# First adaLN sets loaded by feature blocks, and the first four column tiles accumulated as the blocks arrive

## The chip, the cores and the metric

One core of a Trainium2 chip runs the whole program. The metric is the device time of one execution in microseconds, the median of several runs. Two kernels compute the same outputs from the same inputs, and the second differs from the first by one change.

## The reference, cut to what matters

Two layers (`DEPTH = 2`) of a hybrid block with 1024 features run over 256 context tokens and 256 latent tokens. The host passes weights in float32.

```python
for l in range(DEPTH):
    mod = jax.nn.silu(c) @ ada_w[l] + ada_b[l]
    mod_c = jax.nn.silu(c_ctx) @ ada_w[l] + ada_b[l]
    sh1, sc1, g1, sh2, sc2, g2 = jnp.split(mod[:, None, :], 6, axis=-1)
    ...
    h = rms_norm(x, norm_gains[l, 0]) * (1.0 + sc1) + sh1
    hc = rms_norm(xc, norm_gains[l, 0]) * (1.0 + sc1c) + sh1c
    y, y_c = token_mixer(h, hc, ...)
```

`token_mixer` multiplies `h` by `w_in` (1024 x 6576). Columns of the product feed four mixers: a neighbourhood attention (NA), a latent attention (MLA), a gated DeltaNet (GDN) and an S5 state space; the remaining 4096 columns are gates. Each mixer's output is projected, multiplied by its sigmoid gate and summed (`merge_branches`), and a dense MLP follows. Nothing of `h` exists before the first two adaLN sets of the layer, shift `sh1` and scale `sc1`, are known. Each is a product of a conditioning vector with a 1024 x 1024 piece of `ada_w[0]`, for the context and for the latents.

## The kernel before, in words

Context and latents lie side by side as 512 columns (2 x 256), with features on 128 partitions in 8 feature tiles. A **column tile** is 128 columns of `w_in`; its product takes 24 matmuls of 512 columns: 8 feature tiles, and for each three products of split float32 (`mm3`: `whi*hhi`, `whi*hlo`, `wlo*hhi`), accumulated in one PSUM bank. Weights come by DMA as 512 KB `wstage` (3 buffers), ScalarE casts `whi`, VectorE subtracts `wlo` (4 buffers of each). `MIX_ORDER` fixes the order of column tiles in layer 0: u0, u1 (S5's input), nq0, nq1, nk0, nk1, nva, nvb, misc, then eight GDN tiles zipped with gate tiles, the rest of the gates, and MLA's. They are numbered from 0 below, so nk0 is tile 4.

All DMAs named here are issued by SyncE's queue (SP), in program order, and an SP entry that waits holds those behind it. Each other engine runs its own list in order too. Generators (S5's tables, S5, attention, GDN) are advanced by `tick` between column tiles; a scheduler then fixes each engine's list from priorities (`tc.high_priority()` raises one). So the lists below are fixed before the program runs.

**Front.** `first_dma` loads the first two adaLN sets as 16 pieces `ada1` (512 KB, rows of 128 input features each), between them `x` and the constants. `run_ada` accumulates the 8 pieces of a set into one bank (`ada_mm`), and `ada_end` transposes the sum into `mod` and `fac`. So scale, the second set, is there only after the 16th piece. `s5_tables` runs beside it on VectorE (512-column products `raw`, `t`, `sto`), GpSimd (a chain of powers `ph`) and SP. Then `make_h` makes h for the 256 context tokens over all 8 feature tiles, and after that for the 256 latents: VectorE `hb`, ScalarE `hhi`, VectorE `hlo` for each piece of 256 columns.

**Tiles 0 to 3.** `dense_group` takes u0 and u1 in two halves of 256 columns, following the halves of h; the PSUM pool `psd` has two buffers, emptied by ScalarE (`us`, L1425). nq0 and nq1 follow at 512 columns.

**S5.** `ct,bb` matmuls (L717, eight groups) finish the tables in steps; `U,sti` matmuls feed S5's input to its state; VectorE scans it (`tn`, `X`, L998); SP then loads `s5s` (S5's output maps, written to DRAM before by the table code as `s_dr`); `U,s5s` and `Q,s5s` matmuls give its output. Without waits at the list they stand between column tiles on TensorE.

**End of GDN.** The merges of `MERGE = [3, 0, 1, 2]` run over branches S5 (3), NA (0), MLA (1), GDN (2), 8 tiles a branch. GDN's steps (`cv`, `sR,N`, `svn,QK` matmuls with VectorE between) are spread over the gate tiles and merges. Before branch 2 come a sum `oo`, its norm on ScalarE (Square, a table load, Ln, Exp), transposes (L1344) and `yh`. Gates return by DMA into `gin` (3 buffers), ScalarE takes their tanh, VectorE multiplies by the projection, GpSimd adds to `macc`. `NA_AT = [6, 12]` is the number of gate tiles after which a layer's attentions begin to be emitted.

## Time and profile before

| | |
|---|---|
| times of three runs | 1705.52, 1707.88, 1708.6 us, median 1707.88 |
| profiled execution | 1704.83 us, of which the span is 1703.0 |
| mean granted TensorE clock | 0.962 of full speed |
| busy, share of the span | TensorE 93%, VectorE 63%, ScalarE 47%, GpSimd 13% |
| chain that ended last | TensorE 76%, VectorE 10%, DMA 7%, ScalarE 3% |

TensorE's weight loads overlap its matmuls and are listed as PEld. In the page's slices of the span TensorE shows 6 tenths in the first slice, 9 in most, and 7 in the slice that holds the end of layer 0's GDN. A timeline row has start, duration, engine, line, operation and, in brackets, the idle time before it with what ended it.

### The profile page before, as it was taken

The page shows a single profiled execution, that of the slowest core. Times are in us where ns is not written, and L with a number is a line of the kernel's source. Part 1 is how long each engine was busy: PE and PEld are TensorE (multiplying, and loading weights), DVE is VectorE, ACT ScalarE, POOL GpSimd, SP SyncE. Part 2 cuts the span into 40 slices and gives each one's busy share as a digit, 9 for nine tenths or more (in the row PEclk, how much of TensorE's full clock was granted, in tenths as well). Part 3 has the DMA queues.
Part 4 walks back from the last instruction along what each step waited for, and adds up shares of the span by engine and source line. Part 5 has one row for each costly group of instructions (what it writes and reads, how often), then busy time and mean ns, then how long its engine had stood idle before and what let it go on. Part 6 is the DMA issues. An engine that isn't in the chain of part 4 may idle for free.

```text
span 1703.0 us, 25390 instructions
## 1 busy us (share of the span) xinstructions
PE 1591.6 (93%) x9616; PEld 1321.3 (78%) x9616; DVE 1075.1 (63%) x1942; ACT 802.2 (47%) x1491; POOL 221.2 (13%) x316
## 2 busy tenths in 40 slices
PE   6699999999999888999999999789999998889996
PEld 2588777766778778878777878589998877779996
DVE  8766544574456767746757676756677557665554
ACT  5444456533334344534334453556545434556553
POOL 6830000000001454000010050100000002000000
PEclk9799999999999889999999999899999999889998
DMA  8456533445346523346545765334677316736652
GB/s 328 144 140 203 170 124 96 127 155 164 96 136 214 187 98 127 102 137 195 179 136 180 223 188 153 117 105 123 207 241 199 97 38 192 234 114 184 187 186 81
DMA packets 135915, 268.42 MB, mean 158 GB/s; under 512 B 38129, under 2 KB 76017, under 8 KB 135665
## 3 DMA queue, kind: packets, MB, share of 16 engines
q1 hardware_dynamic: 135792, 266.80, 50.1%
q8 instruction: 75, 1.23, 0.3%
q14 instruction: 48, 0.39, 0.1%
HBM read 234.02 MB, written 32.74 MB: 157 GB/s over the span
## 4 chain that ended last, share of the span: by engine, by line
PE 76%; DVE 10%; DMA 7%; ACT 3%; issue 2%; POOL 1%; SPq 0%; POOLq 0%; ACTq 0%; DVEq 0%
PE pd L215 40%; PE pm L215 24%; PE pg L215 9%; DVE wlo L204 2%; DMA gin<-g_dr 2%; DMA wstage<-in_ada 2%; PE pm L833 1%; DMA wstage<-in_win 1%; ACT whi L222 1%; DVE hlo L207 1%; POOL macc L204 1%; PE pd L378 1%; DVE aacc L207 1%; DMA s5s<-s_dr 1%; DMA ys<-yb_dr 1%
## 5 line engine op out<-in xcount | busy, mean ns | idle before, releaser
L204 DVE TENSOR_TENSOR wlo<-wstage,whi 128x1024 fp32r<-128x1024 f32 x264 | 327.4, 1241 | 244.0 <-ACT whi L222 236.0
L222 ACT CAST whi<-wstage 128x1024 fp32r<-128x1024 f32 x264 | 276.3, 1048 | 414.1 <-PE pd L215 163.1
L215 PE MATMUL pd<-hhi,whi 128*128 128x256 f32 (+1 forms) x1184 | 411.1, 348 | 22.7 <-ACT us L1425 10.0
L215 PE MATMUL pd<-hlo,whi 128*128 128x256 f32 (+1 forms) x1184 | 406.0, 343 | 2.8 <-DVE hlo L207 2.8
L215 PE MATMUL pd<-hhi,wlo 128*128 128x256 f32 (+1 forms) x1184 | 406.4, 344 | 0.0
L215 PEld LDWEIGHTS pd<-hhi,whi 128*128 128x128 f32 x1184 | 228.2, 193 | 61.2 <-ACT us L1425 10.2
L215 PEld LDWEIGHTS pd<-hlo,whi 128*128 128x128 f32 x1184 | 228.0, 193 | 33.5 <-issue 6.3
L215 PEld LDWEIGHTS pd<-hhi,wlo 128*128 128x128 f32 x1184 | 227.8, 192 | 31.5 <-issue 8.2
L215 PE MATMUL pm<-hhi,whi 128*128 128x256 f32 (+1 forms) x352 | 115.4, 328 | 5.6 <-ACT hhi L201 5.6
L215 PE MATMUL pm<-hlo,whi 128*128 128x256 f32 (+1 forms) x352 | 115.9, 329 | 2.6 <-DVE hlo L207 2.5
L215 PE MATMUL pm<-hhi,wlo 128*128 128x256 f32 (+1 forms) x352 | 114.7, 326 | 0.0
L207 DVE SCALAR_TENSOR_TENSOR aacc<-wstage,csl,aacc 128x1024 f32<-128x1024 f32 x63 | 81.9, 1320 | 19.8 <-DMA wstage<-in_ada 19.7
L215 PE MATMUL pd<-fhi,whi 128*128 128x256 f32 (+1 forms) x272 | 90.5, 333 | 2.4 <-DVE y L204 2.4
L215 PE MATMUL pd<-fhi,wlo 128*128 128x256 f32 (+1 forms) x272 | 90.4, 332 | 1.2 <-DVE wlo L204 1.2
L215 PE MATMUL pm<-fhi,whi 128*128 128x256 f32 (+1 forms) x272 | 90.1, 331 | 0.0
L215 PE MATMUL pd<-flo,whi 128*128 128x256 f32 (+1 forms) x272 | 90.0, 331 | 0.0
L215 PE MATMUL pm<-flo,whi 128*128 128x256 f32 (+1 forms) x272 | 89.4, 329 | 0.2 <-DVE flo L204 0.2
L215 PE MATMUL pm<-fhi,wlo 128*128 128x256 f32 (+1 forms) x272 | 89.3, 328 | 0.0
L215 PEld LDWEIGHTS pm<-hhi,whi 128*128 128x128 f32 x352 | 68.6, 195 | 13.6 <-ACT hhi L201 6.8
L215 PEld LDWEIGHTS pm<-hlo,whi 128*128 128x128 f32 x352 | 68.1, 194 | 9.6 <-DVE hlo L207 3.7
L215 PEld LDWEIGHTS pm<-hhi,wlo 128*128 128x128 f32 x352 | 68.1, 193 | 5.0
L215 PEld LDWEIGHTS pd<-fhi,whi 128*128 128x128 f32 x272 | 51.9, 191 | 7.7 <-issue 2.8
(588 smaller groups left out, 2881.9 us busy)
## 6 DMA issues: line engine op xcount, KB each, us to landing
wstage<-in_w SPq DMA_DIRECT2D x128, 512.0 KB, 4.2
wstage<-in_win SPq DMA_DIRECT2D x104, 512.0 KB, 4.1
wstage<-in_ada SPq DMA_DIRECT2D x80, 512.0 KB, 3.6
ada<-in_ada SPq DMA_DIRECT2D x16, 512.0 KB, 10.6
g_dr<-gt SPq DMA_DIRECT2D x32, 256.0 KB, 4.2
gin<-g_dr SPq DMA_DIRECT2D x16, 512.0 KB, 4.4
wstage<-in_wb SPq DMA_DIRECT2D x16, 512.0 KB, 4.1
wstage<-in_wout SPq DMA_DIRECT2D x16, 512.0 KB, 3.8
```

Source lines behind the costliest of these rows:

```text
L204: return (eng or V).tensor_tensor(o, a, b, op=op)
L207: return (eng or V).scalar_tensor_tensor(o, a, s, b, op0=op0, op1=op1)
L215: return PE.matmul(o, l, r, start=st, stop=sp)
L222: S.copy(hi, src)
L378: PE.matmul(ps[32 * q:32 * q + 32, 0:256], lhs, w[:, 256 * q:256 * q + 256], start=st, stop=sp)
L833: PE.transpose(ps[:, 128 * b:128 * b + 128], P[qt][:, 128 * b:128 * b + 128], ident)
```

## The change

The host passes a second copy of the two sets, `ada0`: 8 blocks of 1 MB. Block t holds shift and scale of feature tile t, for all 1024 input features. `cond_block(t)` multiplies a block by the conditioning vectors (8 matmuls into four partition quarters, 256 columns), copies the result on ScalarE (`ade`), adds the quarters and turns them by two matmuls with `sel2`, and two small VectorE instructions write `mod` and `fac` of tile t alone. So h can be made feature tile by feature tile, both halves at once, and `make_h` is called so. Tiles 0 to 3 (`NPRE`) get their PSUM banks early and take their three matmuls of a feature tile once it is there, with a lag (`LAG`) of 0, 0, 1 and 2 feature tiles. `x` is now loaded first; the S5 constants `bct` behind the first block and two `wstage`; five buffers hold blocks. The constants `cst` come in two loads. `NA_AT` goes from 6 to 10 in layer 0. After the layer's merges the order of TensorE's list is nearly the same in both.

```diff
+    a0 = g["ada_w"][0, :, 0:2048].reshape(8, 128, 2, 8, 128)
+    o["ada0"] = a0.transpose(3, 1, 0, 2, 4).reshape(8, 128, 2048)
...
-NA_AT = [6, 12]
+NA_AT = [10, 12]
...
-        jobs = [("ada", 0, 8 * s + k) for s in (0, 1) for k in range(8)]
+        jobs = []
...
-            if j < 16:
-
-                if k == 0:
-                    acc_a[0] = ada_ps()
-                ada_mm(acc_a[0], cs[:, k, :], w, k == 0, k == 7)
-                if k == 7:
-                    ada_end(l, s, acc_a[0])
-            elif (l, s) in ((0, 2), (0, 3), (0, 4), (1, 5)):
+            w = stage.pop(j)
...
-            for t in range(8):
+            for t in tiles:
...
-        first = {}
-        def first_dma(n):
-            while n and len(first) < 16:
-                j = len(first)
-                first[j] = px.tile([128, 1024], F32, name="ada1", tag="ada1", bufs=13)
-                SP.dma_start(first[j], I["ada"][0, jobs[j][2]])
-                n -= 1
+        SP.dma_start(smp, I["smp"].rearrange("l p n -> p l n"))
         xt = px.tile([128, 8, 512], F32, name="xt")
-        first_dma(1)
-        SP.dma_start(smp, I["smp"].rearrange("l p n -> p l n"))
+        for c0 in (0, 256):
+            SP.dma_start(xt[:, :, c0:c0 + 256], I["x"][:, :, c0:c0 + 256])
+        SP.dma_start(cst[:, 0:C_BONE], I["cst"][:, 0:C_BONE])
+        blocks = []
+        def block_dma():
+            t = px.tile([128, 8, 256], F32, name="adab", tag="adab", bufs=5)
+            SP.dma_start(t.rearrange("p k f -> p (k f)"), I["ada0"][len(blocks)])
+            blocks.append(t)
+        def cond_block(t):
+            w = blocks[t]
+            ps = ada_ps()
+            for k in range(8):
+                q = k % 4
+                PE.matmul(ps[32 * q:32 * q + 32, 0:256], cs[:, k, :], w[:, k], start=k < 4, stop=k >= 4)
+            e = px.tile([128, 256], F32, name="ade", tag="ade", bufs=2)
+            S.copy(e, ps[:, 0:256])
+            ps = ada_ps()
+            for s in range(2):
+                PE.matmul(ps[:, 2 * s:2 * s + 2], e[:, 128 * s:128 * s + 128], sel2, start=True, stop=True)
+            b = smp[:, 0, P_AB + t:P_AB + t + 16:8]
+            tt(mod[0][:, 0:2, t], ps[:, 0:4].rearrange("p (s c) -> p s c", s=2), b[:, :, None].to_broadcast([128, 2, 2]), ADD)
+            stt(fac[0][:, 0, t], mod[0][:, 1, t], 1.0, smp[:, 0, P_G + t:P_G + t + 1].to_broadcast([128, 2]), ADD, MUL)
...
+        block_dma()
+        issue_dma()
+        issue_dma()
         next(tables)
-        first_dma(1)
-        SP.dma_start(cst, I["cst"][:, 0:C_RO])
-        first_dma(2)
-        SP.dma_start(xt[:, :, 0:256], I["x"][:, :, 0:256])
-        first_dma(2)
-        SP.dma_start(xt[:, :, 256:512], I["x"][:, :, 256:512])
-        first_dma(7)
+        block_dma()
+        issue_dma()
+        block_dma()
...
+        tab = ln_table()
+        rs = []
+        with tc.high_priority():
+            for c0, n, sel in halves(0):
+                rs.append(x_rstd(xt, c0, n, px, tab))
+            sel2 = small.tile([128, 2], F32, name="sel2", tag="sel2", bufs=1)
+            V.tensor_reduce(sel2, ident.rearrange("p (q c) -> p c q", q=4)[:, 0:2, :], axis=AX, op=ADD)
         next(tables)
-        rs = []
-        tab = ln_table()
-        for j in range(16):
-            run_ada(j, first[j])
-            first_dma(1)
-            if j in (5, 9):
-                c0, n, sel = halves(0)[len(rs)]
+        NPRE, LAG = 4, (0, 0, 1, 2)
+        pre = {}
+        for t in range(8 + 1 + max(LAG)):
+            if t < 8:
                 with tc.high_priority():
-                    rs.append(x_rstd(xt, c0, n, px, tab))
-            if j > 5:
-                next(tables)
-        pos[0] = nstage[0] = nsplit[0] = 16
-        for _ in range(3):
-            issue_dma()
-        for c0, n, sel in halves(0):
-            with tc.high_priority():
-                make_h(0, xt, rs[sel], 0, c0, n, sel, px)
+                    cond_block(t)
+                    for c0, n, sel in halves(0):
+                        make_h(0, xt, rs[sel], 0, c0, n, sel, px, (t,))
+            for i in range(NPRE):
+                k = t - 1 - LAG[i]
+                if k == 0:
+                    prep_to(i)
+                    pool_, nm_ = (psd, "pd") if i < 2 else (psm, "pm")
+                    pre[i] = pool_.tile([128, 512], F32, name=nm_, tag=nm_)
+                if 0 <= k < 8:
+                    whi, wlo = parts[i]
+                    mm3(pre[i], whi[:, 128 * k:128 * k + 128], wlo[:, 128 * k:128 * k + 128],
+                        hhi[:, k], hlo[:, k], k == 0, k == 7)
+            while len(blocks) < min(8, t + 4):
+                block_dma()
+            if t == 6:
+                SP.dma_start(cst[:, C_BONE:], I["cst"][:, C_BONE:C_RO])
+            next(tables)
+        for i in range(NPRE):
+            parts.pop(i)
+        pos[0] = NPRE
...
+                ps = pre.pop(order.index(j)) if l == 0 and order.index(j) in pre else dense(key, hhi, hlo, n)
...
+                elif nm == "u0" and l == 0:
+                    for i in range(2):
+                        ps = pre.pop(i)
+                        for sel in range(2):
+                            store_u(i, sel, ps[:, 256 * sel:256 * sel + 256])
```

**TensorE while h is being made.** Before, 256-column matmuls of one tile after the other (`pd`), with S5's `ct,bb` among them:

```order
L215 MATMUL pd<-hhi,wlo 128x256
L717 MATMUL pm<-ct,bb 32x240 x4
L215 MATMUL pd<-hhi,whi 128x256
L215 MATMUL pd<-hlo,whi 128x256
L215 MATMUL pd<-hhi,wlo 128x256
L215 MATMUL pd<-hhi,whi 128x256
L215 MATMUL pd<-hlo,whi 128x256
L215 MATMUL pd<-hhi,wlo 128x256
```

Now, for one feature tile, tiles 0 and 1 (`pd`) and 2 and 3 (`pm`) in turn at 512 columns; `raw` belongs to S5's tables, `sel_313,ade` to a block:

```order
L1370 MATMUL pg<-sel_313,ade 128x2 x2
L671 MATMUL pm<-cst,raw 128x128 x4
L218 MATMUL pd<-hhi,whi 128x512 x2
L218 MATMUL pm<-hhi,whi 128x512 x2
L218 MATMUL pd<-hlo,whi 128x512
L218 MATMUL pd<-hhi,wlo 128x512
L218 MATMUL pd<-hlo,whi 128x512
L218 MATMUL pd<-hhi,wlo 128x512
L218 MATMUL pm<-hlo,whi 128x512
L218 MATMUL pm<-hhi,wlo 128x512
L218 MATMUL pm<-hlo,whi 128x512
L218 MATMUL pm<-hhi,wlo 128x512
```

The four tiles now advance together, and behind VectorE's last `hlo` stand eight matmuls of 512 columns until tile 4; before, 24 matmuls of 256 columns for each of u0 and u1, and then the whole of tiles 2 and 3, stood behind the last pieces of h. The first group of `ct,bb` moved from the start of tile 0 to a place just ahead of the eighth feature tile.

**TensorE at S5's input.** Before, the first of two groups of `U,sti` stands in tile 7:

```order
L215 MATMUL pd<-whi,hhi 128x256
L717 MATMUL pm<-ct,bb 32x240
L215 MATMUL pm<-U,sti 128x64 x16
L717 MATMUL pm<-ct,bb 32x240 x3
L215 MATMUL pd<-wlo,hhi 128x256
```

Now both groups stand at the end of tile 10:

```order
L218 MATMUL pd<-hhi,whi 128x512
L709 MATMUL pm<-ct,bb 32x240
L218 MATMUL pm<-U,sti 128x64 x16
L709 MATMUL pm<-ct,bb 32x240 x3
L218 MATMUL pd<-hlo,whi 128x512
L218 MATMUL pd<-hhi,wlo 128x512
L218 MATMUL pd<-hhi,whi 128x512
L218 MATMUL pd<-hlo,whi 128x512
L218 MATMUL pd<-hhi,wlo 128x512
L218 MATMUL pm<-U,sti 128x64 x16
L709 MATMUL pm<-ct,bb 32x240 x4
```

Counted in column tiles of 24 matmuls, the first group moved from 7.40 to 10.79 and the second from 7.96 to 11.0. The first group of `Q,s5s` moved from 12.67 to 13.0. SP's first `s5s` load waits in both lists for the last `X` of VectorE's scan. Ahead of tile 4 of the new list stands one of the eight `ct,bb` groups, and five more stand between there and the first `U,sti`.

**ScalarE at the end of layer 0's GDN.** Before, the norm follows the last gate's tanh with one table load:

```order
L201 ACTIVATE gin<-gin 128x1024 x2
L201 ACTIVATE oo_3394<-oo_3393 128x1024
L247 ACT_TABLE_LOAD
L201 ACTIVATE orr<-orr,kc 128x16
L201 ACTIVATE orr<-orr 128x16
L222 CAST yh<-ring 128x512 x2
L222 CAST whi<-wstage 128x1024
```

Now a gate's tanh (`gin`) stands between the Square of `oo` and the norm:

```order
L204 ACTIVATE gin<-gin 128x1024
L204 ACTIVATE oo_3375<-oo_3374 128x1024
L250 ACT_TABLE_LOAD
L204 ACT_TABLE_LOAD
L204 ACTIVATE gin<-gin 128x1024
L204 ACT_TABLE_LOAD
L204 ACTIVATE orr<-orr,kc 128x16
L204 ACT_TABLE_LOAD
L204 ACTIVATE orr<-orr 128x16
L225 CAST yh<-ring 128x512 x2
L225 CAST whi<-wstage 128x1024
```

There are four table loads where one was, and three of them stand behind the DMA that loads that gate. Of GDN's matmuls behind the merges of branches 3, 0 and 1, 8 `cv`, 8 `sR,N` and 8 more (4 and 4) `svn,QK` moved ahead of the last of those merges; 4 `svn,QK` are left behind it. In the front, ScalarE has seven table loads where it had three.

## Rows read from the trace of the kernel before

**Rows 1.** Engine line of the page, then ten-microsecond windows: engines' busy time (instructions), clock, DMA
```profile
PE 1591.6 (93%) x9616; PEld 1321.3 (78%) x9616; DVE 1075.1 (63%) x1942; ACT 802.2 (47%) x1491; POOL 221.2 (13%) x316
...
50.00:60.00 10.00, 4.94 (x35) 4.30 (x34) 10.00 (x22) 4.44 (x9) 9.47 (x20) 0.84 0.21 69
60.00:70.00 10.00, 3.92 (x18) 3.92 (x19) 6.44 (x9) 3.19 (x7) 7.20 (x7) 0.50 0.42 138
```

**Rows 2.** What TensorE waited for, 0 to 400 us: total, times, longest
```profile
PE pd L215 <- ACT us L1425: 10.0, 1, 10.0
```

**Rows 3.** TensorE in time: start, us, operation, idle before and its releaser
```profile
66.08 0.58 PE L215 MATMUL pd<-hhi,whi 128*128 128x256 f32 x1 [10.01 <-ACT us L1425]
...
70.89 0.28 PE L215 MATMUL pd<-hlo,whi 128*128 128x256 f32 x1
...
81.11 0.40 PE L215 MATMUL pd<-hlo,whi 128*128 128x512 f32 x1
...
82.32 0.39 PE L215 MATMUL pd<-hhi,whi 128*128 128x512 f32 x1
...
86.45 0.39 PE L215 MATMUL pd<-hhi,whi 128*128 128x512 f32 x1
```

**Rows 4.** VectorE's last piece of h, and one ScalarE hhi behind it, in time
```profile
65.90 0.47 DVE L207 SCALAR_TENSOR_TENSOR hlo<-hb__755,mod,hhi 128x256 fp32r<-128x256 f32 x1
...
48.72 0.51 ACT L201 ACTIVATE hhi<-hb__707,mod 128x256 fp32r<-128x256 f32 x1 [1.22 <-DVE hb__707 L207]
```

**Rows 5.** AdaLN matmuls of the first two sets alone, four windows, their sum
```profile
sum 40.00, PE 9.92 PEld 2.59; mean PE 2.48 PEld 0.65
```

**Rows 6.** TensorE in time: S5's input matmuls, S5's output matmuls, the 14th column tile
```profile
107.93 3.79 PE L215 MATMUL pm<-U,sti 128*128 128x64 f32 x32
...
146.26 0.33 PE L215 MATMUL pm<-U,s5s 128*128 128x64 f32 x2
...
148.86 0.48 PE L215 MATMUL pd<-hlo,whi 128*128 128x512 f32 x1
...
150.78 0.39 PE L215 MATMUL pd<-hhi,whi 128*128 128x512 f32 x1
```

**Rows 7.** VectorE's scan of S5, first and last; SP; s5s, time to landing
```profile
114.06 2.36 DVE L204 TENSOR_TENSOR tn<-X,ph 128x1024 f32<-128x1024 f32 x2 [0.31 <-ACT X L970]
...
137.61 1.29 DVE L204 TENSOR_TENSOR X<-tn 128x512 f32<-128x512 f32 x2
...
139.00 0.98 SPq L956 DMA_DIRECT2D s5s<-s_dr  x2
...
DMA to landing us min/median/max: 3.2/3.8/5.0
```

**Rows 8.** TensorE in time: a GDN step among merges, and the end of GDN
```profile
544.24 1.89 PE L215 MATMUL pg<-sR,N 128*128 128x64 f32 x16
...
575.72 0.40 PE L215 MATMUL pd<-yh,wlo 128*128 128x512 f32 x1
...
600.95 0.79 PE L215 MATMUL pm<-yh,whi 128*128 128x512 f32 x1 [0.64 <-ACT yh L222]
```

**Rows 9.** ScalarE in time at the end of GDN
```profile
594.05 1.06 ACT L201 ACTIVATE oo<-oo 128x1024 f32<-128x1024 f32 x1 [3.20 <-DVE oo L204]
595.12 1.28 ACT L247 ACT_TABLE_LOAD   x1
596.41 0.31 ACT L201 ACTIVATE orr<-orr,kc 128x16 f32<-128x16 f32 x1
596.75 0.21 ACT L201 ACTIVATE orr<-orr 128x16 f32<-128x16 f32 x1
```

**Rows 10.** GpSimd, SP and ScalarE in time: gated branch outputs and gate loads
```profile
580.92 4.72 POOL L204 TENSOR_TENSOR macc<-macc,gin 128x512 f32<-128x512 f32 x3 [4.57 <-DVE gin L207]
...
582.22 3.76 SPq L1552 DMA_DIRECT2D gin<-g_dr  x2
...
585.96 1.06 ACT L201 ACTIVATE gin<-gin 128x1024 f32<-128x1024 f32 x1 [5.64 <-DMA gin<-g_dr]
```

More of the change, by code (lines that the diff above doesn't have):

```diff
@@ L369, in issue_dma @@
             stage[j] = t
-        acc_a, aacc, later, st_px = {}, [], [], [None]
+        aacc, later, st_px = [], [], [None]
         def ada_ps():
@@ L395, in ada_end, with run_ada @@
                     tt(fac[l][:, gi[1]], mod[l][:, s], gb, MUL)
-        def run_ada(j, w=None):
+        def run_ada(j):
             _, l, sk = jobs[j]
             s, k = sk // 8, sk % 8
-            ahead = w is None
-            if ahead:
-                w = stage.pop(j)
-            end = None
-            if j < 16:
-                if k == 0:
-                    acc_a[0] = ada_ps()
-                ada_mm(acc_a[0], cs[:, k, :], w, k == 0, k == 7)
-                if k == 7:
-                    ada_end(l, s, acc_a[0])
-            elif (l, s) in ((0, 2), (0, 3), (0, 4), (1, 5)):
+            w = stage.pop(j)
+            if (l, s) in ((0, 2), (0, 3), (0, 4), (1, 5)):
                 ps = psd.tile([128, 512], F32, name="pd", tag="pd")
@@ L439, in run_ada @@
                     later.append([2, end])
-            if ahead:
-                issue_dma()
+            issue_dma()
         def prep_to(t):
@@ L759, in x_rstd, with make_h @@
             return rs
-        def make_h(l, xt, rs, which, c0, n, sel, tp):
+        def make_h(l, xt, rs, which, c0, n, sel, tp, tiles=range(8)):
             f, sh = fac[l][:, (0, 2)[which]], mod[l][:, (0, 3)[which]]
-            for t in range(8):
+            for t in tiles:
                 b = tp.tile([128, 256], F32, name="hb_", tag="hb_", bufs=3)
@@ L1354, in _emit @@
         SP.dma_start(cc, I["cc"])
-        first = {}
-        def first_dma(n):
-            while n and len(first) < 16:
-                j = len(first)
-                first[j] = px.tile([128, 1024], F32, name="ada1", tag="ada1", bufs=13)
-                SP.dma_start(first[j], I["ada"][0, jobs[j][2]])
-                n -= 1
-        xt = px.tile([128, 8, 512], F32, name="xt")
-        first_dma(1)
-        SP.dma_start(smp, I["smp"].rearrange("l p n -> p l n"))
+        SP.dma_start(smp, I["smp"].rearrange("l p n -> p l n"))
+        xt = px.tile([128, 8, 512], F32, name="xt")
+        for c0 in (0, 256):
[20 more added lines that the diff above has]
+            stt(fac[0][:, 0, t], mod[0][:, 1, t], 1.0, smp[:, 0, P_G + t:P_G + t + 1].to_broadcast([128, 2]), ADD, MUL)
         maps_in = []
         tables = s5_tables(0, pt, maps_in)
+        block_dma()
+        issue_dma()
+        issue_dma()
         next(tables)
-        first_dma(1)
-        SP.dma_start(cst, I["cst"][:, 0:C_RO])
-        first_dma(2)
-        SP.dma_start(xt[:, :, 0:256], I["x"][:, :, 0:256])
-        first_dma(2)
-        SP.dma_start(xt[:, :, 256:512], I["x"][:, :, 256:512])
-        first_dma(7)
+        block_dma()
+        issue_dma()
+        block_dma()
         V.memset(cs, 0.0)
@@ L1452, in win_job @@
                 n = 256 if lat else 512
-                ps = dense(key, hhi, hlo, n)
+                ps = pre.pop(order.index(j)) if l == 0 and order.index(j) in pre else dense(key, hhi, hlo, n)
                 if nm in ("nq0", "nq1", "nk0", "nk1"):
@@ L1668, in _emit @@
             pf.close()
-_SHAPES = {"x": (128, 8, 512), "cc": (128, 8, 2), "cst": (128, C_END), "ada": (L, 48, 128, 1024),
+_SHAPES = {"x": (128, 8, 512), "cc": (128, 8, 2), "cst": (128, C_END), "ada0": (8, 128, 2048), "ada": (L, 48, 128, 1024),
            "win": (L, 52, 128, 1024), "wb": (L, 8, 128, 1024),
```

1 line of the change is left out of this document (removed).

## The prediction

> **What bounds the kernel now.** I read the page's engine line first: TensorE is busy for 1591.6 us, 93% of the span [rows 1]. A change can pay by what TensorE loses, so its waits come next. Up to 400 us the largest is one of 10.0 us for ScalarE's `us` copy [rows 2]. The wait of 10.0 us ends at 66.08, where the second halves of u0 and u1 start [rows 3]. ScalarE is only the messenger there: in its list the `us` copy stands behind the last `hhi`, and that waits for VectorE. The windows show VectorE busy for all of 50 to 60 us, and its last piece of h runs from 65.90 [rows 1, 4]. So VectorE ends the front: it makes h and S5's tables at the same time. Tile 4 starts at 86.45. From 82.32 to there stand 18 matmuls of 512 columns, 0.229 us each, so a column tile takes 24 x 0.229 = 5.5 us [rows 3]. From 81.11 to 82.32 two of them and a group of `ct,bb` take 1.21 us, so the group costs 0.75. The other place is the end of layer 0's GDN: the merges of three branches end at 575.72 + 0.40 = 576.1, and GDN's branch starts at 600.95 [rows 8]. These 24.85 us are a chain of VectorE, TensorE and ScalarE.
>
> **The front up to tile 4.** VectorE has the same 32 pieces of h, 27 table products of 512 columns and four `wlo` ahead of the last piece in both lists. Two transposes go and 16 very small instructions come, and its start depends on `bct`, which is loaded later; I let these cancel, since h can now begin on the first block. So the last piece ends near 66.4, as before (65.90 + 0.47). The blocks cost TensorE no more than the pieces did, 9.9 us in all [rows 5], and most of the first four tiles is done beside VectorE. Eight matmuls, 1.8 us, stand behind the last piece; their `us` copy and cast give little more. Tile 4 starts at about **68.5** (67 to 73, if TensorE is behind when h ends): a lead of 18 us on 86.45.
>
> **What becomes of the lead.** S5's input matmuls moved from 7.40 to 10.79 tiles. Before, they began 107.93 - 86.45 = 21.5 us behind tile 4's start [rows 3, 6]: 3.40 tiles make 18.7 us, and three groups of `ct,bb` and the first matmuls of a fourth the rest. Now 6.79 tiles, five groups and the start of a sixth are 37.2 + 4.1 = 41.3 us, so they begin at 68.5 + 41.3 = 109.8, 1.9 us later than before although tile 4 is 18 us ahead. They take 3.8 us, until 113.6. From there a chain runs that the change does not shorten: in the old trace from 111.7 over VectorE's first `tn` at 114.06 to the end of its last `X` at 138.9, 27.2 us [rows 6, 7]. One `wlo` fewer stands among it, so I take 26.4: 140.0. SP issues `s5s` right behind it, as at 139.00, and it lands 3.8 to 5.0 us later [rows 7]; with the issue, TensorE can have it at about 144.6. Before, only 4.7 tiles and the rest of the inputs lay between, which TensorE filled: it did not wait there. Now there are 2.2 tiles. TensorE arrives at 109.8 + 8.2 (both input groups) + 12.1 + about 1.7 (a short wait on a PSUM buffer) = 131.8 and **waits 12.8 us**. The lead turns into that wait. The output matmuls take 2.6 us (146.26 to 148.86) [rows 6].
>
> A wait is followed by slow matmuls: in the window behind the 10 us wait the granted clock is 0.50, half speed, 1.2 of 2.4 GHz [rows 1]. From 66.08 to 70.89 the old trace has 22 matmuls of 256 columns, 4.81 us, which at full speed (0.118 each) take 2.6 [rows 3]. So I add 2.2 us. Tile 13 starts as if at 144.6 + 2.6 + 2.2 = 149.4, against 150.78 [rows 6]. **Front: 1.4 us gained**, from +2.9 (tile 4 at 67) to -3.1 (at 73).
>
> **The end of GDN.** 24 of 28 small matmuls move ahead of the merges' end. Eight of them show as 16 records, 1.89 us among the merges at full clock [rows 8], so 48 records cost 5.7 us that was inside the tail and now is ahead of it. The tail itself then hangs on a gate. Behind the last merge matmul VectorE needs 1.1 us, GpSimd one or two products of 4.72 / 3 = 1.6, the gate's DMA 3.7 (582.22 to 585.96) to 4.1 [rows 10]: 6.4 to 8.4 us, say 7.4. Then ScalarE does a load of 1.28, the tanh 1.06, a load, 0.31, a load, 0.21: 5.4 us [rows 9, 10]. From the start of the last 0.21 to TensorE's restart the old trace has 600.95 - 596.75 = 4.2, that is 4.0 behind its end [rows 8, 9]. The sum is 16.8 against 24.85, so 8.0 less. **Tail: 8.0 - 5.7 = 2.3 us gained** (1 to 3.5). Four more table loads in the front, 5.1 us on ScalarE, I cost at nothing: it idles there, as before its `hhi` [rows 4]; without that cover they would delay the first piece of h, and VectorE's table products would fill in.
>
> GDN's steps, moved forward by up to two tiles, could make TensorE wait between them. The old trace shows none on such a step, and a gain by order alone has no mechanism here, so I bound this by 0 and -4 and take -0.5. Moving the attentions (`NA_AT`) changes no amount of work; it lies among the same tiles.
>
> The sum is 1.4 + 2.3 - 0.5 = **3.2 us gained**. The profiled execution took 1704.8 us, 3.1 less than the median 1707.9; from the median it gives **1705**, with -6 to +6.4 us of gain from the bounds: 1701.5 to 1714.
>
> **A rule on table loads.** In the trace a load takes 1.28 us, begins 0.01 us behind the Square that ends at 595.11 and is followed by Ln at 596.41 without a gap [rows 9]. The Trainium skill, page "ScalarE: Activation LUTs", section "What ACT_TABLE_LOAD costs", gives about 1.28 us for the load and about 1.38 us more for a drain at each switch. The row agrees with the first figure and shows no room for the second. By the page's figure three more loads in the tail would cost an estimated 4.1 us above my sum.
>
> **Rivals.**
> (a) *The lead is carried whole*, faster: S5's chain does not gate TensorE, for instance since the scan starts earlier or `s5s` is loaded earlier. Tile 13 would start at 68.5 + 49.3 (nine tiles) + 4.5 (six `ct,bb`) + 7.6 + 2.6 = 132.5, 18.3 us ahead; with 2.3 from the tail **1687**. For it speaks that SP waited on another queue entry just ahead of 139.00; against it, that the load waits for the last `X` in both lists, and that the input matmuls moved.
> (b) *The table loads hold ScalarE longer than their bars*: three in the tail at twice the bar, 3 x 1.28 = 3.8 us, take the tail's gain: **1708.5**. Against it stand the rows at 595.12 and 596.41 [rows 9]; they show only one load in one place.
> (c) *Slower: h in step with the blocks holds VectorE up.* Each feature tile now crosses from TensorE to ScalarE, TensorE, VectorE, ScalarE and back to VectorE. Where such a crossing is not covered it costs like the 1.22 us that ScalarE waited for `hb` at 48.72 [rows 4]; eight tiles make 9.8 us. Since tile 4's start carries to the S5 inputs and through their chain one for one, the front would end 8.4 us behind the old one: gain -8.4 + 2.3 - 0.5, **1714.5**. It decides from a tile 4 later than about 70, where the front starts to lose. For it: VectorE's list is in order, with one block's `mod` ahead of the next tile's pieces. Against it: table products stand between to fill.
>
> **How the numbers follow.** About 0.2%, 3.4 us, is what a measurement of this kernel can tell from no change. My forecast has 0.62, of which 0.30 lies faster than that, 0.24 within and 0.08 slower, since the sum stands at the edge and its bounds go both ways. (a) has 0.14, all faster; (b) 0.08, of it 0.07 within; (c) 0.16, slower. That makes faster 0.44, same 0.31, slower 0.25. The range 1692 to 1713 leaves out most of (a) and half of (c).
>
> **What would show it.** Right: tile 4 near 68.5; one TensorE wait of about 10 to 13 us for `s5s` in front of the first output matmuls; tile 13 between 147 and 151; the merge of GDN's branch about 17 us behind the other merges' end, with a gate's DMA ahead of three table loads. Wrong: no such wait (a); the last `hlo` beyond 70 us with VectorE idle before `mod` or `hlo` (c); gaps around the table loads (b); TensorE waits on `cv`, `sR` or `svn` among the gates and merges.

## The result, and the profile after

The changed kernel takes 1715.7 us against 1708.2 us for the kernel before on the same chip: a ratio of 1.0056, interval 1.0037 to 1.0074, so 0.56% slower. The forecast was 1705, range 1692 to 1713. Run 15, the changed kernel measured a second time, gave 1.0066 (1.0047 to 1.0085).

The profiled execution of the changed kernel took 1718.3 us and that of before 1704.8, so the traces stand 13.5 us apart and the medians 7.5. I therefore follow the difference along the program: the column tiles of the dense products (24 matmuls of 512 columns) are counted in both traces and their starts subtracted. Plus is later than before.

| start of column tile | 4 | 8 | 12 | 13 | 14 | 24 | 38 | 59 | 120 | 203 |
|---|---|---|---|---|---|---|---|---|---|---|
| before, us | 86.5 | 119.9 | 142.6 | 150.8 | 159.0 | 228.7 | 367.3 | 609.2 | 982.2 | 1681.5 |
| after, difference | -11.9 | -19.3 | -6.8 | +5.4 | +7.9 | +7.9 | +7.3 | +9.2 | +10.1 | +13.8 |
| after, a second trace | -12.0 | -18.8 | -4.8 | +7.4 | +8.6 | +8.7 | +8.2 | +7.7 | +8.7 | +9.7 |

(At tile 8 the kernel before has run the S5 input groups already and the changed one has not.) The lead at tile 4 is real. Between tiles 12 and 14 it turns into a lag of 7.9 us (8.6 in the second trace), as large as the whole loss. Layer 0 from there on adds 1.3 us in one trace and gives back 1.0 in the other. Behind tile 120 one trace of the changed kernel loses 3.7 us more and the other 1.0. Between tiles 126 and 156 all 18 other traces of this document, that of run 7 (the kernel before with one constant changed) among them, lose 2.6 to 9.3 us on this one trace of before, so that stretch says something of this trace and not of the change; I draw nothing from that part.

The page's engine line of after, and below it ten-microsecond windows (length; busy us of TensorE, its weight loads, VectorE, ScalarE and GpSimd; granted clock; share and GB/s of the DMA engines):

```profile
PE 1588.8 (93%) x9600; PEld 1315.2 (77%) x9600; DVE 1072.8 (62%) x1954; ACT 810.8 (47%) x1502; POOL 215.9 (13%) x316
```

```profile
50.00:60.00 10.00, 10.00 (x76) 7.63 (x75) 6.30 (x10) 3.34 (x8) 9.45 (x18) 1.00 0.01 2
...
140.00:150.00 10.00, 1.54 (x7) 0.94 (x5) 9.93 (x24) 3.44 (x6) 0.00 (x0) 0.71 0.28 86
150.00:160.00 10.00, 8.88 (x33) 8.14 (x34) 5.19 (x12) 2.22 (x4) 0.00 (x0) 0.50 0.61 206
```

TensorE is full from 50 to 60 us, where it stood half idle before, and VectorE is busy for 6.3 us there instead of 10.0. The hole is now at 140 to 150 us, where TensorE has 1.5 us of work, and behind it the clock is 0.50. What TensorE waited for from 0 to 400 us, and VectorE from 10 to 72 us (total, times, longest):

```profile
PE pm L218 <- DMA s5s<-s_dr: 9.6, 1, 9.6
...
DVE mod L207 <- PE pg L1370: 6.2, 5, 3.6
```

The wait of 10.0 us for the `us` copy [rows 2] is gone, and one of 9.6 us for `s5s` has come. (A longer one, 12.3 us for the constants, ends ahead of TensorE's first matmul.) VectorE now waits 6.2 us for the small matmuls that give `mod`. The same in time, TensorE, then VectorE, then SP:

```profile
74.54 0.50 PE L218 MATMUL pd<-hhi,whi 128*128 128x512 f32 x1
...
118.71 3.79 PE L218 MATMUL pm<-U,sti 128*128 128x64 f32 x32
...
151.12 0.66 PE L218 MATMUL pm<-U,s5s 128*128 128x64 f32 x2 [9.58 <-DMA s5s<-s_dr]
...
156.23 0.77 PE L218 MATMUL pd<-hhi,whi 128*128 128x512 f32 x1
156.80 0.63 PE L218 MATMUL pd<-hlo,whi 128*128 128x512 f32 x1
157.23 0.63 PE L218 MATMUL pd<-hhi,wlo 128*128 128x512 f32 x1
...
161.40 0.39 PE L218 MATMUL pd<-hhi,whi 128*128 128x512 f32 x1
161.63 0.40 PE L218 MATMUL pd<-hlo,whi 128*128 128x512 f32 x1
...
55.18 0.16 DVE L207 TENSOR_TENSOR mod<-pg,smp 128x4 f32<-128x4 f32 x1 [3.63 <-PE pg L1370]
...
71.42 0.48 DVE L210 SCALAR_TENSOR_TENSOR hlo<-hb__829,mod,hhi 128x256 fp32r<-128x256 f32 x1
...
124.83 2.36 DVE L207 TENSOR_TENSOR tn<-X,ph 128x1024 f32<-128x1024 f32 x2 [8.82 <-ACT X L962]
...
146.44 1.28 DVE L207 TENSOR_TENSOR X<-tn 128x512 f32<-128x512 f32 x2
...
147.75 6.55 SPq L948 DMA_DIRECT2D s5s<-s_dr  x3
```

Tile 4's first matmul is at 74.54 against 86.45 [rows 3]; the input groups start at 118.71 against 107.93 [rows 6]; VectorE's last `X` starts at 146.44 against 137.61 [rows 7]. From 156.80 to 161.07 a matmul of 512 columns takes 0.43 us, from 161.40 on 0.23. So S5's chain ends 8.8 us later than before although tile 4 is 12 us earlier, and tile 13 starts at 156.23 against 150.78 [rows 6].

The end of GDN, TensorE and then ScalarE:

```profile
591.79 0.40 PE L218 MATMUL pd<-yh,wlo 128*128 128x512 f32 x1
...
608.14 1.94 PE L1336 MATMUL pg<-cst,oo 128*128 128x128 f32 x8 [15.12 <-DVE oo L207]
610.72 0.80 PE L218 MATMUL pm<-yh,whi 128*128 128x512 f32 x1 [0.64 <-ACT yh L225]
...
598.88 1.06 ACT L204 ACTIVATE oo<-oo 128x1024 f32<-128x1024 f32 x1
599.95 1.28 ACT L250 ACT_TABLE_LOAD   x1
601.24 1.28 ACT L204 ACT_TABLE_LOAD   x1
602.53 1.06 ACT L204 ACTIVATE gin<-gin 128x1024 f32<-128x1024 f32 x1
603.61 1.28 ACT L204 ACT_TABLE_LOAD   x1
604.90 0.31 ACT L204 ACTIVATE orr<-orr,kc 128x16 f32<-128x16 f32 x1
605.23 1.28 ACT L204 ACT_TABLE_LOAD   x1
606.52 0.22 ACT L204 ACTIVATE orr<-orr 128x16 f32<-128x16 f32 x1
```

From the merges' end, 591.79 + 0.40 = 592.2, to the restart at 610.72 are 18.5 us, where the kernel before had 24.85 [rows 8].

### The profile page after: what moved, and what is told of

The parts are those of the page before. It is cut to its first block, busy times and chain, and to the rows that moved or that the text cites. A ratio compares the mean times of both kernels' runs of the same rounds, so it can differ in the third digit from the quotient of the medians.

```text
span 1716.5 us, 25387 instructions
## 1 busy us (share of the span) xinstructions
PE 1588.8 (93%) x9600; PEld 1315.2 (77%) x9600; DVE 1072.8 (62%) x1954; ACT 810.8 (47%) x1502; POOL 215.9 (13%) x316
## 4 chain that ended last, share of the span: by engine, by line
PE 72%; DVE 9%; DMA 9%; ACT 4%; issue 2%; SPq 1%; POOL 1%; POOLq 0%; ACTq 0%; DVEq 0%
PE pd L218 37%; PE pm L218 24%; PE pg L218 8%; DVE wlo L207 2%; DMA wstage<-in_win 2%; DMA wstage<-in_w 1%; DMA gin<-g_dr 1%; ACT whi L225 1%; PE pm L825 1%; POOL macc L207 1%; PE pd L381 1%; DMA wstage<-in_wb 1%; ACT L204 1%; DMA wstage<-in_ada 1%; DMA cst<-in_cst 1%
## 5 line engine op out<-in xcount | busy, mean ns | idle before, releaser
L218 PE MATMUL pd<-hhi,whi 128*128 128x512 f32 (+1 forms) x1152 | 401.0, 349 | 15.2 <-ACT gt L1511 5.7
L218 PE MATMUL pd<-hlo,whi 128*128 128x512 f32 (+1 forms) x1152 | 397.0, 345 | 0.0
L218 PE MATMUL pd<-hhi,wlo 128*128 128x512 f32 (+1 forms) x1152 | 396.6, 344 | 0.0
L218 PEld LDWEIGHTS pd<-hhi,whi 128*128 128x128 f32 x1152 | 220.1, 192 | 54.3 <-issue 9.0
L218 PEld LDWEIGHTS pd<-hhi,wlo 128*128 128x128 f32 x1152 | 219.5, 191 | 35.8 <-issue 12.3
L218 PEld LDWEIGHTS pd<-hlo,whi 128*128 128x128 f32 x1152 | 220.2, 191 | 30.0 <-issue 6.9
L218 PE MATMUL pm<-hhi,whi 128*128 128x256 f32 (+1 forms) x368 | 120.2, 329 | 7.1 <-ACT hhi L204 5.7
L218 PE MATMUL pm<-hlo,whi 128*128 128x256 f32 (+1 forms) x368 | 121.0, 329 | 3.1 <-DVE hlo L210 3.1
L218 PE MATMUL pm<-hhi,wlo 128*128 128x256 f32 (+1 forms) x368 | 120.3, 327 | 0.6 <-DVE wlo L207 0.6
L218 PE MATMUL pg<-sqh,cst 128*128 128x256 f32 x112 | 38.7, 480 | 28.1 <-ACT sqh L204 15.8
```

The costliest lines, as they stand in the source:

```text
L218: return PE.matmul(o, l, r, start=st, stop=sp)
```

## The experiments

Ratios are to the kernel before on the same chip. "Tile 24" and "tile 59" are starts of column tiles against the one trace of before (plus is later). A single trace can be some us away from the median of its kernel: at tile 59 that of run 13 stands 5.1 us ahead of that of run 9, and run 13 is not the faster of the two. Theory A: TensorE's wait for `s5s` and its half clock take the lead. Rivals: the chain in front of that load ends when it ends, whoever waits for it (B); the later attentions and the reordered GDN steps (C). Later expectations sharpen these, as A2, A3, B2, C2; each says how.

**1. The output group later, on TensorE alone.**

```diff
+                while l == 0 and q == 0 and at_tile[0] < 15:
+                    yield (0.0, 0.3)
...
+                        after(i, behind)   # first output matmul behind the last dense one
```

> Edit: layer 0's first output group of S5 may only start behind the column tile before tile 15, two tiles later in TensorE's list; nothing else is asked for. Theory A (the early tiles' lead is lost in the wait of 9.6 us for s5s at 151 us and in the half clock behind it, some 5 us): the wait goes, tiles 13 and 14 stand in its place at full clock, and the time falls by 10 to 15 us, to about 1701 to 1706; from column tile 17 on TensorE is ahead of the changed kernel by that much, and the wait for oo in GDN's tail does not take it back. Rival B (the loss is the front, h late by 5.5 us, and S5's chain ends when it ends: what is freed at 151 us is paid again at the later output groups or at GDN): 1713 to 1717. Rival C (the loss comes from the later attentions and the reordered GDN steps): 1713 to 1717 too, with the wait at 151 us gone but the merges' end unchanged.

1.0050 (1.0030 to 1.0069); tile 24 +2.2, tile 59 +4.4. Tiles 24 and 59 come some 5 us earlier than in the changed kernel's first trace, but the time is not told apart from its time; A's 1701 to 1706 did not come. The matmuls moved, the wait stayed. First TensorE, then ScalarE:

```profile
150.76 0.79 PE L218 MATMUL pd<-hhi,whi 128*128 128x512 f32 x1 [9.71 <-ACT ring L1501]
...
143.10 1.05 ACT L1006 COPY Q<-X 64x1024 f32<-64x1024 f32 x1 [7.75 <-DVE ring L1500]
...
149.60 0.63 ACT L204 ACTIVATE ring<-cv 128x512 f32<-128x512 f32 x1 [3.04 <-DVE ring L1500]
```

TensorE now waits 9.7 us for a PSUM buffer. ScalarE empties it (`ring`, L1501), but in its list the `Q` copies stand ahead, and those waited 7.7 us while VectorE scanned; behind them a tanh of `cv` waited 3.0 us more for VectorE, whose `cv` steps stand around the scan's last ones. In the changed kernel both waits are the same (7.75 and 3.03). Moving one engine's list left the others' where they were.

**2. Own buffers for the output maps**, so that `s5s` loads without waiting for the scan's temporaries.

```diff
-                w = tp.tile([128, 2, 3, 128], F32, name="s5s", tag="s5s", bufs=2)
+                w = tp.tile([128, 2, 3, 128], F32, name="s5o", tag="s5o", bufs=2)
```

> Edit: S5's output maps get two buffers of their own in place of the two that they share with the scan's temporaries, so that their load no longer waits for VectorE's last turn; list positions stay. Theory A: the wait at 151 us is the sum of VectorE's chain and of a load of 4 to 5 us behind it; only the load is taken away, the wait shrinks from 9.6 to about 5 us, less half clock behind it: 1709 to 1713. If the chain itself (scan, last turn, ScalarE's Q copies) were nearly as late as the load: no difference, 1714 to 1717. Rivals B and C: 1714 to 1717.

1.0020 (1.0005 to 1.0035). The wait was 4.1 us, for ScalarE's `Q`, as expected; but tile 24 stood at +7.0, so the front gave back 0.9 us only. The rest of the gain lies behind it (tile 59 +5.3) and I can't assign it.

**3, 8. The loading alone**, without early accumulation; in the second run also `NA_AT = [6, 12]`.

```diff
-        NPRE, LAG = 4, (0, 0, 1, 2)
+        NPRE, LAG = 0, (0,)
...
```

> Edit: the blocks stay, h is still made tile by tile as they arrive, but no column tile accumulates early: u0 and u1 run behind h, as before. Theory A: tile 4 starts about 93 us (71.9 plus four tiles), 6 us later than in the kernel before and 19 us later than in the changed one, but S5's input matmuls stand at 8.0 tiles, so they start at about 115, some 4 us earlier than in the changed kernel; the wait for s5s is about 3 to 6 us and the time 1708 to 1716: giving up a 12.6 us lead costs nothing. Rival B (a later front is paid one for one): the lead is worth its 12 to 19 us, so 1727 to 1735. Rival C: 1715 plus or minus 3.

> Edit: blocks and h tile by tile, no early accumulation, attentions at the sixth gate: of the three parts only the loading is left. In the run with the blocks only, the last piece of h ended at 63.8 us (before 66.4, changed 71.9) and column tile 24 came 1.4 us ahead of the kernel before. Theory A2 (early accumulation holds VectorE up and pushes S5's chain back; the loading itself is good): tile 24 1 to 2 us ahead, and without the later attentions' loss the whole is at or below before, ratio 0.997 to 1.001. Rival D (the loading itself costs later, as the median of that run, 1715 us, says): ratio 1.003 to 1.007.

1.0071 (1.0046 to 1.0096) and 1.0003 (0.9980 to 1.0025). VectorE in time in the first one's trace:

```profile
63.35 0.47 DVE L210 SCALAR_TENSOR_TENSOR hlo<-hb__738,mod,hhi 128x256 fp32r<-128x256 f32 x1
...
139.33 1.29 DVE L207 TENSOR_TENSOR X<-tn 128x512 f32<-128x512 f32 x2
```

What VectorE waited for from 10 to 72 us:

```profile
DVE mod L207 <- PE pg L1370: 0.3, 1, 0.3
```

Tile 4 was expected 6 us later than before and came 3.5 earlier. Without the early matmuls VectorE waits 0.3 us for `mod` instead of 6.2, h ends at 63.8 us instead of 71.9, and the last `X` starts at 139.3 instead of 146.4. So it is the early accumulation, in TensorE's list ahead of the next block's matmuls, that holds VectorE up, not the blocks. The second trace, with the same front list, had 66.1 and 145.3, 1.5 us of waits for `mod`, and tile 24 was -1.2 in one and +4.8 in the other: the front of this version is not steady, and the 1 to 2 us ahead that the second was to show did not come. The one constant between the two runs, `NA_AT`, is worth some 11 us here; more on it under 4, 7, 13.

**4, 7, 13. The attentions.** At the sixth gate again in the changed kernel; at the tenth in the kernel before (the diff the other way round); at the sixth in the run with doubled tables (9).

```diff
-NA_AT = [10, 12]
+NA_AT = [6, 12]
```

> Edit: layer 0's attentions start at the sixth gate again, the rest is the changed kernel. Theory A: this part of the change is worth less than its share of TensorE's list, 1713 to 1718; GDN's steps z,N stand one tile later again, so the waits among them (about 3 us) shrink, and the tail behind the merges stays short (about 18 us) if the moved records do it, or returns to about 25 if the attentions do. Rival C (moving the attentions and with them GDN's steps is what costs): 1706 to 1710.

> Edit: the kernel before with layer 0's attentions started at the tenth gate instead of the sixth, nothing else. Theory C1 (starting the attentions later costs by itself, 5 to 6 us as the changed kernel lost by it): ratio 1.003 to 1.004. Theory C2 (it costs only where GDN's steps move forward in TensorE's list with it; here z,N stands within a few tenths of a tile of where it stood, 42 to 48.9): ratio 0.999 to 1.001.

> Edit: the run with the doubled table buffers alone (ratio 0.9994), and layer 0's attentions start at the sixth gate again. Theory A3 with the attentions as a cost of its own (5.8 us between the changed kernel and the run with attentions as before): the region from column tile 24 to 59 gives back some 5 us, ratio 0.995 to 0.998, and the version beats both kernels. Theory C2 (the attentions cost only through the place of GDN's steps; here z,N stand at 41.8 to 49.0 with either): no difference, 0.998 to 1.001.

1.0022 (1.0008 to 1.0036), 0.9997 (0.9981 to 1.0014), 1.0009 (0.9994 to 1.0024). So the later attentions cost some 6 us in the changed kernel and nothing in the other two. Runs 3 and 8 are a fourth such pair, and there they cost most: 1.0071 against 1.0003. In the two without a cost, GDN's `z,N` steps stand at the same column tiles with either setting (42 to 49). In the changed kernel they stand at 41.0 to 47.0, some less than a tile apart, and with the sixth gate at 41.0 to 48.0, one to a tile. Tile 24 (+7.9, +7.8) is equal; tile 59 is +9.2 against +1.8. In the stretch from 500 to 520 us the changed kernel waits 2.6 us for `N` and `tm`, and the other 0.8 us for `rr`. That the place of GDN's steps is the cause fits these three pairs, but those waits are only a part of the 7.4 us, and two runs speak against it: in run 2 the steps stand at 41.0 to 47.0 as in the changed kernel, and its time, 1.0020, is that of run 4; in run 3 they stand at 41.0 to 48.0, one to a tile, as in run 4, and its ratio is the highest of all. The cost is measured in two pairs; its cause is open.

**5. The input groups early**: other PSUM buffers and no pause ahead of them or among them, so that they stand at 6.2 tiles, with the later output group of (1).

```diff
-            yield (0.0, 5.0)
+            yield (0.0, 0.0 if l == 0 else 5.0)
...
-                ps = psm.tile([128, 512], F32, name="pm", tag="pm")
+                ps = ada_ps() if l == 0 else psm.tile([128, 512], F32, name="pm", tag="pm")
...
-                yield (1.8, 0.0)
+                if l == 1:
+                    yield (1.8, 0.0)
```

> Edit: as the run with the later output group, and besides S5's four input groups of layer 0 get PSUM buffers of another pool and no pause among them, so that they stand at 6.2 column tiles in TensorE's list instead of 10.8. In the changed kernel their tables are copied by 68.3 us and U is loaded by 89 us, yet they start at 118.7 us and VectorE idles 8.8 us for their X. Theory A2 (the lead is lost because S5's chain, input matmuls, scan, last turn on VectorE, ends at 146 to 148 us whatever TensorE does, and it does so because its start stands late in TensorE's list): input matmuls at 88 to 92 us, last turn by 120 to 130 us instead of 147.7, no wait above 3 us before column tile 20, column tile 24 at 6 to 12 us ahead of the kernel before (the later-output run: 2.2 us behind). The time then falls by 6 to 12 us against that run, ratio to before 0.996 to 1.001, if GDN does not take it back. Rival B2 (the output tables' own chain, ct and bb to s_dr, is as late): the wait stays at 8 to 12 us under another name, tile 24 within 3 us of the later-output run, ratio 1.004 to 1.007.

1.0059 (1.0036 to 1.0082), tile 24 +8.0: the rival held, though tile 24 came 5.8 us behind run 1 where it allowed 3. TensorE, then VectorE:

```profile
87.06 7.33 PE L218 MATMUL pg<-U,sti 128*128 128x64 f32 x64 [0.32 <-DMA U<-u_dr]
156.82 0.80 PE L218 MATMUL pd<-hhi,whi 128*128 128x512 f32 x1 [7.94 <-ACT ring L1502]
...
124.03 1.29 DVE L207 TENSOR_TENSOR X<-tn 128x512 f32<-128x512 f32 x2
155.65 0.06 DVE L1500 MEMSET ring<- 128x4 f32 x1 [9.66 <-DMA s_dr<-TP]
```

The scan ended 22 us earlier, but it took VectorE from the tables. Their last store ended at 155.65, and GDN's `ring`, whose pool is opened when the tables' pool is closed, waited for it.

**6, 9, 12. The tables faster**: two buffers for `sto` and `ct`; (6) also without the pause ahead of the input groups, (12) with the input groups of (5), the output group behind tile 14 and no priority for the scan.

```diff
-                sto = tp.tile([128, 4, 2, 128], F32, name="sto", tag="sto")
+                sto = tp.tile([128, 4, 2, 128], F32, name="sto", tag="sto", bufs=2 if keep_in is not None else 1)
```

> Edit: the changed kernel with two buffers each for sto and ct in layer 0's tables, and no pause in front of the input groups; TensorE's list then has the input groups at 7.5, 8.9 and 9.8 tiles, the last ct,bb group at 8.9 instead of 11.0, and the output groups from 14.7 on. Theory A2: the chain starts some 10 to 15 us earlier and the output groups stand 1.7 tiles later, so the wait of 9.6 us and its half clock go: tile 24 is 5 to 10 us ahead of the kernel before (changed kernel: 7.5 behind), ratio 0.996 to 1.001. GDN's steps stand at 41.0 to 48.0 as in the run with the attentions as before, which adds some 5 us of gain if theory C2 (the later attentions cost by the place of GDN's steps, 41 to 47 tiles) holds; by the front alone the ratio is 0.998 to 1.002. Rival B2 (another chain is as late): ratio 1.003 to 1.006.

> Edit: the changed kernel with two buffers each for sto and ct in layer 0's tables, the pause in front of the input groups left as it is: one half of the run with the tables doubled, which had ratio 0.9994 and column tile 24 at 3.0 us ahead of the kernel before. Theory A3 (two chains behind h, the output tables' and the scan's, end near 144 to 148 us together, and the tables' chain is as slow as it is since each quarter's products wait for the copies of the quarter before): the gain is from the buffers, so column tile 24 comes 0 to 4 us ahead of before and the ratio is 0.999 to 1.003 (GDN's steps stand at 41.8 to 49 here, as in the run with the later output group, which may add 2 to 5 us). Rival E (the gain came from the inputs' earlier first group): as the changed kernel, tile 24 at 5 to 8 us behind, ratio 1.004 to 1.006.

> Edit: the changed kernel with both chains shortened: doubled table buffers, the four input groups at 6.3 tiles on PSUM buffers of their own, the scan without priority over the tables, the first output group behind column tile 14. Theory A3: neither chain is late any more; the input groups start at 87 to 92 us, the last turn ends by 125 to 135, the last ct,bb group stands at 10.2 tiles (some 115 us), no wait above 3 us between 90 and 200 us; the lead of 12.7 us at tile 4 is mostly carried: tile 24 comes 7 to 13 us ahead of before. Ratio 0.994 to 0.998 if GDN's region keeps it, 0.998 to 1.002 if it costs the 5 to 6 us that the later-output run lost from tile 33 to 59. Rival B2 (another work on VectorE, ScalarE's evictions among it, is late whatever the order): tile 24 within 4 us of before, ratio 1.000 to 1.004.

0.9994 (0.9975 to 1.0013), 0.9994 (0.9981 to 1.0007), 1.0009 (0.9994 to 1.0024); tile 24 -3.0, -6.1, -2.9. The loss is gone. In the trace of (9) the output group runs without a wait, at 14.9 tiles:

```profile
98.98 1.02 PE L709 MATMUL pm<-ct,bb 128*32 128x240 f32 x16 [3.97 <-POOL sto L214]
...
155.91 0.33 PE L218 MATMUL pm<-U,s5s 128*128 128x64 f32 x2
```

Its last `X` starts at 147.2, no earlier than in the changed kernel. So A3's ratio held and its reason did not: the chain ended no earlier, but the output groups stand two tiles later, and ScalarE's and VectorE's steps with them. (12) shortened both chains (last `X` at 124.2) and got no more for it, as its rival said.

**10, 11. The doubled tables without early accumulation**, in the kernel before (11 buffers for `ada1`, to make room) and in the blocks-only version with the attentions as before; both without the pause ahead of the input groups.

> Edit: the kernel before with two buffers each for sto and ct, no pause in front of the input groups, and eleven instead of thirteen buffers for the first adaLN pieces to make room. Theory A3 (what bounds layer 0's mixers up to tile 17 is S5's chain behind h, not the first tiles): the kernel before gains too, since its last ct,bb group goes from 8.0 to 6.1 tiles and the output groups from 12.7 to 11.5 without a new wait; or, as its TensorE did not wait there, it gains nothing at tile 24 (within 2 us of before) and the ratio is 0.997 to 1.001. If it gained as much as the changed kernel did by the same edit (some 10 us at tile 24, ratio 0.993 to 0.995), early accumulation would have no part in the loss. Fewer buffers may cost 1 to 3 us in the front.

> Edit: blocks and h tile by tile, no early accumulation, attentions as before, with the doubled table buffers and no pause. Theory A3: h ends at 64 to 66 us, the table chain starts at once; column tile 24 comes 2 to 8 us ahead of before and the ratio is 0.995 to 1.000: as good as or better than the same tables with early accumulation (0.9994), which would say that early accumulation is worth nothing even with the shorter chain. If early accumulation carries part of its lead once the chain is shorter, this run is 3 to 8 us slower than that one: 1.001 to 1.004.

1.0033 (1.0016 to 1.0050) and 1.0058 (1.0038 to 1.0077), tile 24 +3.5 and +6.7. Here the same edits cost: h ended at 69.6 and 68.5 us, and TensorE had not waited for S5 before, so there was nothing to win. One more `sto` product stands on VectorE ahead of the last piece of h in both, and in (10) it waits 2.1 us for the DMA that empties `sto`; that this is the whole of it is not shown, and (10) has fewer `ada1` buffers too. I had expected neither. With the doubled tables early accumulation is worth 0.5 to 0.6% (1.0058 against 1.0009 of (13) and 0.9994 of (6) and (9); only (6) is without the pause too); with single ones nothing (1.0003 against 1.0022, runs 8 and 4).

**16. The output groups later on all engines**: S5 of layer 0 without its priority, all else as changed.

```diff
-                    s5r = start(s5_mixer(l, st, ps5), 1.0, True)
+                    s5r = start(s5_mixer(l, st, ps5), 1.0, l == 1)
```

> Edit: the changed kernel with S5's scan of layer 0 left without its priority in the order; the tables and their buffers stay single. The input groups stay at 10.8 and 11.0 column tiles, and the output groups move from 13.0 to 14.8 tiles on TensorE with ScalarE's Q copies and VectorE's turns placed to match, which the run with the later output group did on TensorE alone. Theory A (the lead is lost in the wait because the output groups stand too early in the lists): the wait for s5s goes, no wait above 3 us between 90 and 230 us, column tile 24 at 3 to 7 us ahead of before like the run with doubled tables, ratio 0.998 to 1.001. Theory A3 (the chain starts too late, the input groups at 118 us, whatever the place of the output groups): the wait takes another name, ScalarE's ring or gt, as in the run with the later output group: tile 24 at 2 to 7 us behind, ratio 1.002 to 1.005.

0.9995 (0.9980 to 1.0011); tile 24 -3.6, tile 59 -7.1. This settles A against A3: the input groups start at 117.2 us, 1.5 earlier than in the changed kernel, the last `X` ends no earlier, the tables are single, and yet the loss is gone. What TensorE waited for from 130 to 230 us, and below it the start of its first output group and a window:

```profile
PE pd L218 <- ACT ring L1495: 4.7, 2, 3.0
PE pd L218 <- ACT gt L1511: 1.4, 1, 1.4
```

```profile
155.93 0.33 PE L218 MATMUL pm<-U,s5s 128*128 128x64 f32 x2
...
150.00:160.00 10.00, 10.00 (x51) 8.47 (x50) 6.24 (x14) 1.60 (x3) 0.00 (x0) 0.83 0.43 143
```

The groups stand at 14.8 tiles instead of 13.0, so TensorE has two more tiles to do while VectorE scans: it waits 6.1 us in all for ScalarE's evictions, and the clock from 150 to 160 us is 0.83 instead of 0.50. The edit also lets other work of VectorE and ScalarE go ahead of the scan's steps, so what it moves is the whole of the scan's lists and not the output matmuls alone. GDN's `z,N` stand as in run 4 here, which accounts for a part of tile 59, but not of tile 24.

**14, 17. The rest of the tables' waits**: (9) with three of GpSimd's products of the last two quarters on VectorE, then with three buffers for `sto`.

```diff
+                on = None if l == 0 and q > 1 else G
-                rank1(cp[1], pc[:, 0], vc[:, 1], gs, G)
+                rank1(cp[1], pc[:, 0], vc[:, 1], gs, on)
```

> Edit: the run with the doubled table buffers alone, and three of GpSimd's products of each of the last two table quarters run on VectorE, which is busy only 4.7 of 10 us between 90 and 100 us there. Theory A3 (of the lead of 15.2 us at tile 4 that run still loses 8.6 us by tile 24, of it 4.0 us in a wait for GpSimd's sto at 99 us and some 2 us in the half clock behind it): the wait shrinks to below 1 us and tile 24 comes 8 to 12 us ahead of before instead of 6.6; ratio 0.996 to 0.999. Rival B2 (what follows, the evictions behind the scan, ends when it ends): tile 24 at 4 to 8 us ahead, ratio 0.998 to 1.001.

> Edit: the run with GpSimd's products of two table quarters on VectorE (ratio 0.9981), with three buffers for sto instead of two. There VectorE and GpSimd waited for the DMA that empties sto before the third quarter. If that wait still holds the chain: input groups 2 to 4 us earlier, tile 24 at 6 to 9 us ahead (5.0 there), ratio 0.996 to 0.998. If not: 0.997 to 0.9995.

0.9981 (0.9967 to 0.9995) and 0.9988 (0.9975 to 1.0001). The first beats both kernels, by 0.2% and 0.8%. The wait for `sto` fell from 4.0 to 2.1 us and then went. Tile 13 stood at -6.0 and -10.3 (-5.5 in 9), tile 24 at -2.8 and -8.9 (-6.1 in 9). So the products on VectorE moved no start of the front by more than half a microsecond up to tile 13, and the 8 to 12 us that A3 gave tile 24 did not come; the third buffer brought tile 13 forward by 4.3 us, so the emptying of `sto` was what was left there. In time neither is told apart from the other or from (9).

**15. The changed kernel again**, for what repeats.

> Edit: none, the changed kernel a second time, for what its trace repeats. If the loss is settled in layer 0 by the order of the lists: tile 4 at 12 to 13 us and tile 24 at 7 to 8 us from the kernel before again, with the wait for s5s of 9 to 10 us; the step of 5 us between tiles 126 and 156 may come out otherwise. Ratio 1.003 to 1.007.

1.0066, with the wait for `s5s` at 9.5 us; its starts stand in the first table.

## Why the prediction was wrong

The mechanism was named: the lead turns into a wait for `s5s` with half clock behind it, and run 16 shows that this is the loss. What failed are sizes, nearly all one way.

- **Tile 4 at 68.5 (a lead of 18).** It came at 74.5. The step that failed is "these cancel": that VectorE's list holds the same work says nothing of its waits. h ended at 71.9, 5.5 us behind the 66.4 forecast, with 6.2 us of waits for `mod`. That is rival (c), which "decides from a tile 4 later than about 70" and gave 1714.5. It had 0.16; the step should have been priced from the crossings, as the rival was, since early matmuls of the same change stand between them in TensorE's list. Runs 3 and 8, without them, show them as the cause: 0.3 and 1.5 us of such waits, h at 63.8 and 66.1. That 1714.5 lies close to the measured time is luck in part: (c) put 9.8 us on the front up to tile 4, where 6.0 were lost, and left the clock at 2.2.
- **Input groups 41.3 us behind tile 4.** They came 118.7 - 74.5 = 44.2 behind, 2.9 more, of it 1.3 in a wait for VectorE's `vt`. They stood 8.9 us behind the forecast 109.8 in all, and VectorE idled 8.8 us for them.
- **The chain of 31.0 us from there to the load.** It took 28.6 (122.5 to 151.1). The load came at 151.1 instead of 144.6.
- **The wait of 12.8 us.** It was 9.6: TensorE came later too.
- **Half clock, 2.2 us.** The output group took 5.1 us for 2.6, and 12 dense matmuls to 161.40 took 5.2 for 2.75: together 4.9. I had taken the count of matmuls from the old wait [rows 3] and forgotten that the output group itself runs in the slow stretch.
- **Front.** 6.5 for the load and 2.7 for the clock turn the forecast gain of 1.4 into a loss of 7.8; tiles 14 and 24 show 7.9.
- **GDN's tail.** 18.5 against 16.8 forecast. A fourth table load explains 1.28 of it: L250's own load at 599.95 is followed at once by the one for the gate's tanh. The tail gained 6.3 and not 8.0. Ahead of it the lag grew from 7.9 us at tile 24 to 16.1 at the merges' end (592.2 against 576.1), a loss of 8.2 where 5.7 + 0.5 was forecast. Up to GDN's branch the region lost 1.9 us where 1.8 was to be gained; in the second trace it gained 1.2. That `NA_AT` "changes no amount of work" is no reason for zero: it cost 6 and 11 us in two of four pairs (runs 4 and 8), by what is open.
- **Rival (b)** is refuted: each of the four loads starts 0.01 to 0.02 us behind the instruction ahead and ends 0.01 before the next. By the Trainium skill, page "ScalarE: Activation LUTs", section "What ACT_TABLE_LOAD costs", a drain of about 1.38 us comes with each switch; no row here has room for one.
- **Rival (a)**, the lead carried whole, was not seen in any run: the best (17) kept 8.9 of 10.9 us to tile 24, and its time is 0.1% below the kernel before.

What stays open: why the later attentions cost time in the changed kernel and in run 3 and none in the other pairs, and why run 12, with both chains early, keeps no more than run 9.

## What to carry to other kernels

A lead in front of a fixed list is worth what stands in the list between it and the next chain: count the filler in both lists, and move the consumer of the chain later on all engines at once, since a group moved on one engine leaves its copies on another as the next wait. Work put into an engine's idle time also lengthens that engine's answers to others: look for who waits for its small instructions.

## What the hardware showed

Behind the 9.6 us wait TensorE's granted clock was 0.50 (the lower level, 1.2 of 2.4 GHz) for ten microseconds of nearly unbroken work, 151.1 to some 161.1, before it rose; behind the old wait of 10.0 us it had been 22 matmuls of 256 columns in 4.8 us [rows 3]. So the clock added 4.9 us to a wait of 9.6. In run 1, behind a wait of 9.7 us, 12 matmuls of 512 columns ran at the lower level (0.50 granted from 150.76 to 156.00) before it rose.
